# Gate products of a decoder layer: seven block products in place of eight, with keys and values in halves

## Chip, cores and metric

The kernel runs on one core of one Trainium2 chip. The metric is the device time of one execution in microseconds (us); the times shown are the median and the spread of three runs. All times below are in us unless ns is written.

## What is computed

A decoder layer on 2048 tokens of width 1024 in float32: one input projection, two causal mixers side by side, gates, a merge and a layer norm.

```python
h = x @ w_in + b_in          # columns: latents 544, z_a, u, v, z_b 512 each, g_a, g_b 1024 each
y_a = mla_attention(c_q, c_kv, k_pe) * silu(z_a)      # 8 heads, 96 wide for scores, 64 for values
y_b = spatial_gating(u, v) * silu(z_b)                # gelu(u) * (tril(w_s) layer_norm(gelu(v)) + b_s)
merged = sigmoid(g_a) * (y_a @ w_oa) + sigmoid(g_b) * (y_b @ w_ob)
x = layer_norm(2 ** 0.25 * x + merged @ w_out)
```

## The kernel before, in words

Every float32 product runs as three passes: `split` (L64) cuts an operand into a head (`hi`, a cast on ScalarE) and a rest (`lo`, a subtraction on VectorE), and `mm3` (L68) adds hi*hi, hi*lo and lo*hi in PSUM. The function has four stages.

- **Stage 1** makes the latents and q, k, v of 4 chunks of 512 tokens, and puts them in DRAM (`qnd`, `qrd`, `kd`, `krd`, `vd`).
- **Stage 2** makes v of the spatial gating unit (`gelu_v`, L375, tile `psa`), and mixes it (`mix`, L453): products `psm`, transposes `ptu`, copies `mo` on ScalarE, and writes of `mxd` by GpSimd's DMA queue. `mo` has two buffers.
- **The gates** (`gates`, L493): z_a, u, z_b, g_a and g_b are 28 column blocks of 128; each is a product of a 1024 x 128 piece of `w_feat` with x of 512 tokens, for 4 chunks: 28 x 4 groups of 8 k tiles x 3 passes, 2688 matmuls of 128 x 512 into tile `psg`, which has two PSUM banks (L408). `weights` (L496) loads a 512 KB piece (`fst`) and splits it (`fwh`, `fwl`) once for two chunks. `group` (L507) closes a bank after 24 matmuls: VectorE adds the bias (L522), or ScalarE takes the tanh (L518); `finish` (L527) does the rest of gelu and silu, and GpSimd's queue writes `fo` to `gd`. `gates` is a generator: one `next` issues one step of three matmuls. x is on chip for two chunks; `x_pieces` (L126) exchanges it halfway.
- **Stage 3, attention** (L575 to L767) per head and block of 256 queries (`Block`, L593): `score` (tiles of up to 512 keys in four banks `pss`, row maxima on VectorE, exponentials `pr` on ScalarE), `turn` (transposes `pt`, split into `ph` on ScalarE and `pl` on VectorE), `product` (with V into `po`). A loop at L716 sets TensorE's order by a clock of its own: each attention step is issued when what it waits for should be done (the `LAG_` constants, L53), and a step of `gates` (648 ns) goes in whenever no such step is due, or while the gates are owed time (`FILL`, L54). `keep_in_program_order` holds TensorE to that order. 48 gate steps go ahead of attention (L571), the rest of them after it. `head` (L582) loads K and V of a whole head into one of two buffers; a block's Q is loaded one block ahead (`block`, L706). Even heads take their blocks upward, odd heads downward (L696).
- **Stage 4** (from L774) multiplies by the gates, merges, projects by `w_out` and normalises; its first loads (`y`, `zb`, `o`, `z`, `r`) begin once attention has freed its memory, beside the last gate steps.

All loads are issued from SyncE's queue (SP), in order; `gd`, `mxd` and the attention output `otd` are written from GpSimd's queue (POOL).

Of the kernel before, what the change touches and what calls it, by code (L numbers as in the profile page):

```python
# [33 lines left out]
W = 512           # width of each mixer  # L34
C = 512           # tokens of a chunk
# [6 lines left out]
# inv_freq[i] = 10000 ** (-2 i / 32) in float32  # L42
# [15 lines left out]
def hybrid_layer_kernel(ctx, tc, xT, x, pos, invf, w_lat, b_lat, w_v, b_v,  # L58
# [37 lines left out]
    # by chunk: attention before its normalisation, mixed v, gates  # L96
# [5 lines left out]
    # ----------------------------------------------------------- constants  # L102
# [7 lines left out]
    # keep where q - k >= 0  # L110
# [7 lines left out]
    # x^T, two chunks of tokens on chip, each as (hi, lo)  # L118
    xp_cm = tc.tile_pool(name="xp", bufs=2, side="right")
# [4 lines left out]
    xt = {}  # L124

    def x_pieces(c):  # L126
        hi = xp.tile([P, KD, C], F32R, tag="xh", name=f"xh{c}")
        lo = xp.tile([P, KD, C], F32R, tag="xl", name=f"xl{c}")
        xt[c] = (hi, lo)
        for k in range(0, KD, 2):  # L130
            st = xs.tile([P, 2, C], F32, tag="st", name="xst")
            sp.dma_start(st, xT_v[:, k:k + 2, c * C:(c + 1) * C])
            for j in range(2):
                yield
                split(st[:, j, :], hi[:, k + j, :], lo[:, k + j, :])
# [5 lines left out]
    # ======================================================= 1: q, k and v  # L141
# [13 lines left out]
    hi0 = xp.tile([P, KD, C], F32R, tag="xh", name="xh0")  # L155
    lo0 = xp.tile([P, KD, C], F32R, tag="xl", name="xl0")
    for k in range(0, KD, 2):
# [6 lines left out]
        for j in range(2):  # L164
            split(st[:, j, :], hi0[:, k + j, :], lo0[:, k + j, :])
            split(ws[:, j, :], wlh[:, k + j, :], wll[:, k + j, :])
    xt[0] = (hi0, lo0)
# [5 lines left out]
    # rope tables: cos, sin of pos * inv_freq for all tokens  # L173
# [24 lines left out]
    # cos(r) = sin(pi/2 - |r|)  # L198
# [6 lines left out]
    # up projections, with the rms gains (and the score scale) folded in  # L205
# [21 lines left out]
    def rope(dst, src, t0, n, heads, nm):  # L227
        """dst[P, n*heads, 32] = rope(src); tables of token tiles t0 .. t0+n"""
# [16 lines left out]
    def latent(c, ts):  # L245
        """latents of token tiles ts: bias, rms norm, rope of k"""
# [8 lines left out]
        for k, t, h2 in order:  # L255
            tk = slice(t * P, (t + 1) * P)
            cs = slice(h2 * 272, (h2 + 1) * 272)
            mm3(pss[t, h2], (xh[:, k, tk], xl[:, k, tk]),
# [32 lines left out]
    def up(c, lh, ll):  # L291
        """k, v and q of a chunk, in four parts"""
# [16 lines left out]
        for t in range(4):  # L309
            tk = slice(t * P, (t + 1) * P)  # L310
            # q rope
# [8 lines left out]
            # k nope, head pairs  # L320
# [4 lines left out]
            # v  # L325
# [10 lines left out]
            # q nope, head pairs  # L336
# [24 lines left out]
    # ============================== 2: v of the spatial gating unit, mixed  # L361
# [572 lines left out]
```

## Time and profile before

| | |
|---|---|
| time, median of 3 runs (lowest to highest) | 1775.66 us (1775.54 to 1776.54) |
| span of the profiled execution | 1775.5 us |
| TensorE matmul busy | 1731.4 us, 98% |
| VectorE (DVE) busy | 1094.2 us, 62% |
| ScalarE (ACT) busy | 754.6 us, 43% |
| GpSimd (POOL) busy | 134.3 us, 8% |
| DMA | 229.06 MB, mean 129 GB/s |

The profiled execution's span and the median of the runs are 0.2 us apart: what lies around the span is small, and sums made against the span hold for the time. A matmul's shown duration overlaps that of the next, so a busy TensorE can still hide gaps of up to two tenths of a microsecond; the distance from one start to the next is what a matmul costs. Idle time in brackets stands before an instruction, with the one that ended it.

### The profile page before, as it was taken

What the parts mean: (1) busy time and instruction counts of PE and PEld (TensorE: products, weight loads), DVE (VectorE), ACT (ScalarE), POOL (GpSimd) and SP (SyncE); (2) the same over time, 40 slices, a digit from 0 to 9 for tenths busy, and PEclk for the clock granted to TensorE, in tenths of its full rate; (3) what the DMA queues carried; (4) which work ended last, traced back from release to release, by engine and by line L of the source; (5) the groups of instructions that cost most, each with busy time, mean ns of one, the idle gap of its engine ahead of it and who ended that gap; (6) DMA issues with size and microseconds to landing.
All of it is one profiled execution on the core that took longest, in us unless ns stands there. A gap on an engine that the chain in (4) does not pass through costs nothing.

```text
span 1775.5 us, 25048 instructions
## 1 busy us (share of the span) xinstructions
PE 1731.4 (98%) x9249; PEld 1484.1 (84%) x9249; DVE 1094.2 (62%) x2209; ACT 754.6 (43%) x1708; POOL 134.3 (8%) x231
## 2 busy tenths in 40 slices
PE   7999999899999999999999999999999999999998
PEld 7999887788888888888788888888888877888886
DVE  6765686476664555444776666654445478777664
ACT  6533442255544454545655445544544341303020
POOL 0000011100000100000100000100001000000000
PEclk9999999999999999999999999999999999999999
DMA  6564851631321422422713212321123886657341
GB/s 220 194 196 160 276 170 38 181 99 49 101 72 66 140 68 66 119 68 75 215 62 89 76 55 81 122 72 59 60 66 120 283 270 225 215 197 215 120 131 72
DMA packets 111100, 229.06 MB, mean 129 GB/s; under 512 B 13120, under 2 KB 41920, under 8 KB 108608
## 3 DMA queue, kind: packets, MB, share of 16 engines
q1 hardware_dynamic: 99968, 193.88, 34.9%
q0 software_dynamic: 11008, 33.57, 5.4%
q8 instruction: 73, 1.20, 0.3%
q14 instruction: 51, 0.42, 0.1%
HBM read 155.50 MB, written 71.89 MB: 128 GB/s over the span
## 4 chain that ended last, share of the span: by engine, by line
PE 45%; issue 41%; DMA 5%; POOL 4%; DVE 3%; ACT 2%; SPq 0%; POOLq 0%; DVEq 0%; ACTq 0%
PE po L86 11%; PE psg L86 9%; PE psa L86 4%; PE psl L86 4%; PE pb L86 4%; PE pa L86 4%; PE pss L86 3%; PE pt L658 2%; POOL gd L519 2%; DMA wost<-in_w_out_dram 1%; PE psq L86 1%; POOL otd L686 1%; DMA xst<-in_xT_dram 1%; DMA mxd<-mo 1%; PE psr L86 1%
## 5 line engine op out<-in xcount | busy, mean ns | idle before, releaser
L86 PE MATMUL psg<-xh,fwh 128*128 128x512 f32 x896 | 375.3, 419 | 4.9 <-DVE fo L522 4.9
L66 DVE TENSOR_TENSOR pl<-pt,ph 128x512 fp32r<-128x512 f32 (+2 forms) x352 | 199.7, 567 | 287.2 <-ACT ph L65 285.5
L86 PE MATMUL psg<-xl,fwh 128*128 128x512 f32 x896 | 354.5, 396 | 0.0
L86 PE MATMUL psg<-xh,fwl 128*128 128x512 f32 x896 | 354.1, 395 | 0.0
L65 ACT CAST ph<-pt 128x512 fp32r<-128x512 f32 (+2 forms) x352 | 172.0, 489 | 241.4 <-PE pt L658 208.8
L642 ACT ACTIVATE pr<-pss,nm 128x512 f32<-128x512 f32 (+2 forms) x320 | 198.0, 628 | 114.9 <-DVE nm L639 95.9
L86 PE MATMUL pss<-Kh,Q 96*128 96x512 f32 (+3 forms) x640 | 222.5, 377 | 12.9 <-DMA Q<-qrd 7.2
L86 PEld LDWEIGHTS psg<-xh,fwl 128*128 128x128 f32 x896 | 169.6, 189 | 38.4
L636 DVE TENSOR_REDUCE mx<-pss 128x1 f32<-128x384 f32 (+2 forms) x288 | 175.6, 619 | 29.4 <-PE pss L86 26.1
L86 PEld LDWEIGHTS psg<-xh,fwh 128*128 128x128 f32 x896 | 170.6, 190 | 25.6 <-issue 5.3
L86 PEld LDWEIGHTS psg<-xl,fwh 128*128 128x128 f32 x896 | 171.4, 191 | 20.7
L658 PE MATMUL pt<-ident,pr 128*128 128x128 f32 x1088 | 167.2, 274 | 0.0
L86 PEld LDWEIGHTS pss<-Kh,Q 96*128 96x128 f32 x640 | 119.3, 189 | 30.7 <-ACT pr L642 9.7
L658 PEld LDWEIGHTS pt<-ident,pr 128*128 128x128 f32 x1088 | 125.6, 141 | 5.8 <-ACT pr L642 0.4
L86 PEld LDWEIGHTS po<-ph,V 128*128 128x128 f32 x576 | 108.7, 189 | 26.0 <-ACT ph L65 3.2
L86 PE MATMUL pss<-Kl,Q 96*128 96x512 f32 (+2 forms) x320 | 115.9, 362 | 0.0
L86 PE MATMUL po<-pl,V 128*128 128x256 f32 x576 | 113.9, 279 | 0.2
L86 PE MATMUL po<-ph,V 128*128 128x256 f32 x576 | 112.8, 276 | 1.2 <-DVE o L685 0.7
L86 PEld LDWEIGHTS po<-pl,V 128*128 128x128 f32 x576 | 96.5, 190 | 11.3 <-DVE pl L66 1.2
L86 PE MATMUL po<-woh,mh 128*128 128x512 f32 x256 | 100.8, 394 | 1.2 <-ACT mh L65 1.2
L86 PE MATMUL po<-woh,ml 128*128 128x512 f32 x256 | 100.4, 393 | 0.0
L86 PE MATMUL po<-wol,mh 128*128 128x512 f32 x256 | 99.7, 390 | 0.0
(208 smaller groups left out, 2986.3 us busy)
## 6 DMA issues: line engine op xcount, KB each, us to landing
fst<-in_w_feat_dram SPq DMA_DIRECT2D x56, 512.0 KB, 3.7
gd<-fo POOLq DMA_DIRECT2D x96, 256.0 KB, 2.3
wabst<-in_w_ab_dram SPq DMA_DIRECT2D x32, 512.0 KB, 4.2
xst<-in_xT_dram SPq DMA_DIRECT2D x31, 512.0 KB, 4.9
kd<-e SPq DMA_DIRECT2D x16, 512.0 KB, 3.2
vd<-ve SPq DMA_DIRECT2D x16, 512.0 KB, 4.1
qnd<-e SPq DMA_DIRECT2D x16, 512.0 KB, 4.7
Q<-qnd SPq DMA_DIRECT2D x64, 128.0 KB, 2.9
```

Of the source, the lines that this page charges most:

```text
L65: act.copy(hi, src)
L66: dve.tensor_tensor(lo, src, hi.bitcast(F32), op=ALU.subtract)
L86: inorder(pe.matmul(*args, **kw))
L519: pool.dma_start(gd[c][m], o)
L636: dve.tensor_reduce(self.mx[:, i:i + 1], ps[:, :n], axis=AX.X, op=ALU.max)
L642: act.activation(pr[:, k0:k0 + ne], pe_[:, :ne], AF.Exp, bias=self.nm, accum_out=ls[:, self.h, 2 * self.qc + j, e:e + 1])
L658: inorder(pe.transpose(pt[:, i, j * P:(j + 1) * P], self.pr[j][:, (k + i) * P:(k + i + 1) * P], ident))
L686: pool.dma_start(otd[self.qc // 2][self.h * DV:(self.h + 1) * DV, self.qc % 2 * 256:(self.qc % 2 + 1) * 256], o2)
```

## The change

The 28 column blocks are paired into 14 units, and a unit, two halves of the 1024-long contraction and two chunks of tokens make 2 x 2 blocks on either side of the product. Sums and differences of blocks of the weights (p6, p3, p7) and of x (T1 to T4) give the four results by seven block products instead of eight, with three partial sums p1, p1+p6 and p1+p6+p5. For each pair of chunks (two passes `p`) there are two sweeps over the units: z=0 makes p1, p6, p5, p3 in one bank, one on top of the other, copies the three partial sums out to DRAM (`rawd`) and finishes one result; z=1 makes p7, p4 and p2, and adds the partial sum that it loads back. Two units alternate on the two banks. A block product is 4 k tiles x 3 passes, 12 matmuls: 14 x 2 x 7 x 12 = 2352.

K and V are loaded in halves of the keys (the second half has one buffer), Q has three buffers and comes two blocks ahead, all heads take their blocks upward, a row's score tiles end at key 1024, and u is no longer multiplied by z_b on the way: stage 4 loads `u` and multiplies.

```diff
-MT_ORDER = [m for f in range(4) for m in (MT_U + f, MT_ZB + f, MT_ZA + f)] + list(range(MT_GA, MT))
-FILL = 1.19       # time of the gates' products per time of the attention's
+_UZ = [m for f in range(4) for m in (MT_U + f, MT_ZB + f, MT_ZA + f)]
+_GM = list(range(MT_GA, MT))
+UNITS = [(m, _GM[n]) for n, m in enumerate(_UZ)] + [(_GM[12], _GM[13]), (_GM[14], _GM[15])]
+UNITS = UNITS[:6] + UNITS[12:13] + UNITS[6:12] + UNITS[13:]
+FILL = 1.03
+    rawd = [[dram.tile([3, P, C], F32, name=f"rw{p}_{n}") for n in range(MT // 2)] for p in range(2)]
...
+    def x_sum(p, what, slot, of=None):
...
+        for k in range(4):
+            a, b = nxt
+            if k < 3:
+                nxt = fetch(k + 1)
+            v = a[:, 0]
+            if what == "T1":
+                dve.tensor_tensor(v, a[:, 1], v, op=ALU.subtract)
+            elif what == "T3":
+                dve.tensor_tensor(v, v, a[:, 1], op=ALU.subtract)
+            elif b is not None:
+                dve.tensor_tensor(v, v, b[:, 1], op=ALU.subtract)
+                dve.tensor_tensor(v, v, b[:, 0], op=ALU.add)
+            elif what in ("T2", "T4"):
+                for e in xc[p, {"T2": "T1", "T4": "T2"}[what]]:
+                    dve.tensor_tensor(v, v, e[:, k, :].bitcast(F32), op=ALU.subtract)
+            split(v, hl[0][:, k, :], hl[1][:, k, :])
+            yield
...
+        def load(p, z, n, e):
+            m1, m2 = UNITS[2 * n + e]
+            st = []
+            for m in (m1, m2):
+                t = fw.tile([P, KD, P], F32, tag="fst", bufs=4, name="fst")
+                sp.dma_start(t, w_feat[m])
...
+            elif q == "p6":
+                dve.tensor_tensor(a22, a22, a21, op=ALU.add)
+                yield
+                dve.tensor_tensor(a21, a22, a11, op=ALU.subtract)
+                cut(key, a21)
...
+            if q in ("p1", "p6", "p5"):
+                o = fq[0].tile([P, C], F32, tag="fo", bufs=3, name="fo")
+                act.copy(o, ps)
+                pool.dma_start(rawd[p][u][("p1", "p6", "p5").index(q)], o)
+                return
...
+            else:
+                m, c = {"p2": (m1, c1), "p4": (m2, c1), "p7": (m2, c2)}[q]
+                o = kept.pop(key)
+                if m < MT_GA:
+                    dve.scalar_tensor_tensor(o, ps, bft[:, m:m + 1], o, op0=ALU.add, op1=ALU.add)
+                else:
+                    dve.tensor_tensor(o, ps, o, op=ALU.add)
...
+            if i + 3 < len(prods):
+                jobs = prepare(prods[i + 3])
...
+                    t = fq[0].tile([P, C], F32, tag="fo", bufs=3, name="fo")
+                    sp.dma_start(t, rawd[pp_][2 * n4 + e4][{"p2": 0, "p4": 1, "p7": 2}[q4[4]]])
...
+            if i + 5 < len(prods) and prods[i + 5][4] == PASS[prods[i + 5][1]][0]:
+                load(*prods[i + 5][:4])
...
+        first = gates(fw, fq, ps_g)
+        next(first)
         mix(*pend)
...
+    fq_cm = tc.tile_pool(name="fq", bufs=2, side="right")
+    fq.append(fq_cm.__enter__())
+    for _ in range(47):
         next(fill)
...
-        order = [(h, qc if h % 2 == 0 else 7 - qc) for h in range(H) for qc in range(8)]
+        order = [(h, qc) for h in range(H) for qc in range(8)]
...
-                if n % 8 == 1 and h + 1 < H:
-                    hds[h + 1] = head(h + 1)
+                if qc == 2:
+                    hds[h, 1] = head(h, 1)
+                if qc == 4 and h + 1 < H:
+                    hds[h + 1, 0] = head(h + 1, 0)
...
+                u = wa.tile([P, C], F32, tag="r", name="u")
+                sp.dma_start(u, gd[c][MT_U + f])
                 dve.tensor_tensor(y, y, z, op=ALU.mult)
+                dve.tensor_tensor(y, y, u, op=ALU.mult)
```

Counted over the built programs: gate matmuls 2688 to 2352; loads of `fst` 56 to 112; splits of weights (`fwh`, `fwl`) 112 to 196; new on VectorE 112 sums of weight blocks, 48 sums of x, and 84 additions that close a bank (against 48 biases before); splits of x 64 to 96; new on ScalarE 84 copies that close a bank, and 24 with the bias; new on GpSimd's queue 84 writes of `rawd` and 16 of `gd`; new on SP 84 loads of `rawd`. The score tiles have the same number of columns in all, 24 more matmuls of them are 128 wide, and 48 more are 256 wide.

The order on TensorE at the end of stage 2 (`ptu` is the last transpose of the mixing, `psg` with its number a bank's use by one group or unit). Before:

```order
L472 MATMUL ptu_3511<-ident_78,um_3454 128x128 x4
L472 MATMUL ptu_3519<-ident_78,um_3454 128x128 x4
L86 MATMUL psg_3573<-xl1_2967,fwh_3535 128x512
L86 MATMUL psg_3573<-xh1_2966,fwl_3536 128x512
L86 MATMUL psg_3573<-xh1_2966,fwh_3535 128x512
...
L86 MATMUL psg_3615<-xh0_2940,fwh_3609 128x512
```

Now:

```order
L90 MATMUL psg_3632<-xh0_2976,fwh_3536 128x512
L90 MATMUL psg_3632<-xl0_2977,fwh_3536 128x512
...
L708 MATMUL ptu_3607<-ident_106,um_3550 128x128 x4
L708 MATMUL ptu_3615<-ident_106,um_3550 128x128 x4
L90 MATMUL psg_3632<-xh1_3304,fwh_3546 128x512
L90 MATMUL psg_3632<-xl1_3305,fwh_3546 128x512
```

Before, groups with banks of their own followed the last transpose; now the first product after it (p6) adds into the bank that p1 has filled ahead of it, which is to be copied out first.

The order on VectorE amid attention (`pl` is attention's split, `mx` and `nm` its maxima; `fst`, `fwl` and `fo` are the gates'). Before:

```order
L66 TENSOR_TENSOR pl<-pt,ph 128x512
L636 TENSOR_REDUCE mx<-pss 128x1
L522 TENSOR_SCALAR fo<-psg,bft 128x512
L66 TENSOR_TENSOR fwl<-fst,fwh 128x512 x2
L545 SCALAR_TENSOR_TENSOR fo<-ft,fo 128x512
L66 TENSOR_TENSOR pl<-pt,ph 128x512
L547 TENSOR_TENSOR fo<-fo,gu 128x512
```

Now:

```order
L70 TENSOR_TENSOR fwl<-fst,fwh 128x512
L70 TENSOR_TENSOR pl<-pt,ph 128x512
L455 TENSOR_TENSOR fst<-fst 128x512
L457 TENSOR_TENSOR fst<-fst 128x512
L455 TENSOR_TENSOR fst<-fst 128x512
L462 TENSOR_TENSOR fst<-fst 128x512
L70 TENSOR_TENSOR pl<-pt,ph 128x512
L522 TENSOR_TENSOR fo<-psg,fo 128x512
L70 TENSOR_TENSOR fwl<-fst,fwh 128x512
```

Sums of freshly loaded weights now stand between attention's splits.

The order on SP at a change of heads (`Kl`, `Kh`, `V` are a head's keys and values). Before:

```order
L588 DMA Kl_10012<-kd_59 64x2048
L588 DMA Kh_10011<-kd_59 64x2048
L589 DMA Kh_10011<-krd_60 32x2048
L589 DMA Kl_10012<-krd_60 32x2048
L603 DMA Q_10019<-qnd_57 64x2x256
```

Now:

```order
L759 DMA Kl_6816<-krd_60 32x1024
L437 DMA fst_6517<-in_w_feat_dram 128x1024
L758 DMA Kh_6375<-kd_59 64x1024
L759 DMA Kh_6375<-krd_60 32x1024
L758 DMA Kl_6376<-kd_59 64x1024
L759 DMA Kl_6376<-krd_60 32x1024
L773 DMA Q_6383<-qnd_57 64x2x256
```

The weights' loads now stand between the halves of K.

## Rows read from the trace of the kernel before

**Rows 1.** Time windows: PE, PEld, DVE, ACT, POOL busy (instructions), TensorE clock, DMA share, GB/s.

```profile
307.00:1412.00 1105.00, 1085.28 (x5934) 937.92 (x5933) 633.24 (x1275) 546.53 (x1326) 91.41 (x167) 0.99 0.32 98
339.00:1366.00 1027.00, 1011.85 (x5591) 877.85 (x5591) 595.66 (x1213) 522.76 (x1287) 81.96 (x150) 0.99 0.28 86
```

**Rows 2.** Timeline of PE, gate matmuls: start, duration.

```profile
329.76 0.39 PE L86 MATMUL psg<-xh,fwl 128*128 128x512 f32 x1
...
334.52 0.39 PE L86 MATMUL psg<-xh,fwl 128*128 128x512 f32 x1
...
644.41 0.40 PE L86 MATMUL psg<-xh,fwl 128*128 128x512 f32 x1
...
645.80 0.39 PE L86 MATMUL psg<-xh,fwl 128*128 128x512 f32 x1
```

**Rows 3.** Timeline of PE, the end of stage 2.

```profile
319.65 1.14 PE L472 MATMUL ptu<-ident,um 128*128 128x128 f32 x8
...
339.77 0.76 PE L86 MATMUL psg<-xh,fwh 128*128 128x512 f32 x1 [4.87 <-DVE fo L522]
340.34 0.63 PE L86 MATMUL psg<-xl,fwh 128*128 128x512 f32 x1
...
345.03 0.63 PE L86 MATMUL psg<-xh,fwh 128*128 128x512 f32 x1
```

**Rows 4.** Chain that ended last, the same place.

```profile
326.86 10.82 DMA mxd<-mo
```

**Rows 5.** Waits: who for whom, us in total, times, longest.

```profile
DVE pl L66 <- ACT ph L65: 285.5, 199, 2.3
...
DVE ls L691 <- DMA mxd<-mo: 8.5, 1, 8.5
...
PE pss L86 <- DMA Q<-qrd: 7.2, 3, 3.1
```

**Rows 6.** Timeline of PE at a change of heads.

```profile
611.56 0.41 PE L86 MATMUL pss<-Kh,Q 96*128 96x384 f32 x1 [3.13 <-DMA Q<-qrd]
...
613.50 0.63 PE L86 MATMUL psg<-xh,fwh 128*128 128x512 f32 x1
613.93 0.63 PE L86 MATMUL psg<-xl,fwh 128*128 128x512 f32 x1
```

**Rows 7.** Groups by line, VectorE: count | busy us, mean ns | idle before.

```profile
L66 DVE TENSOR_TENSOR pl<-pt,ph 128x512 fp32r<-128x512 f32 x224 | 154.5, 690 | 227.6 <-ACT ph L65 226.5
L66 DVE TENSOR_TENSOR fwl<-fst,fwh 128x512 fp32r<-128x512 f32 x112 | 75.1, 686 | 28.1 <-ACT fwh L65 27.7
L522 DVE TENSOR_SCALAR fo<-psg,bft 128x512 f32<-128x512 f32 x48 | 35.9, 748 | 18.1 <-PE psg L86 17.2
```

**Rows 8.** Groups by line, ScalarE.

```profile
L65 ACT CAST fwh<-fst 128x512 fp32r<-128x512 f32 x112 | 66.7, 622 | 38.0 <-PE psg L86 37.6 <-DMA fst<-in_w_feat_dram 0.4
L518 ACT ACTIVATE fo<-psg,bfh 128x512 f32<-128x512 f32 x64 | 44.2, 690 | 26.3 <-PE psg L86 26.3
L474 ACT COPY mo<-ptu 128x512 f32<-128x512 f32 x16 | 9.0, 587 | 23.5 <-PE ptu L472 15.9 <-DMA mxd<-mo 7.6
```

**Rows 9.** Time windows of 10 us amid attention, columns as in rows 1.

```profile
860.00:870.00 10.00, 8.80 (x48) 7.55 (x49) 7.68 (x20) 6.03 (x17) 1.13 (x3) 1.00 1.01 344
870.00:880.00 10.00, 10.00 (x57) 8.57 (x56) 9.36 (x22) 9.75 (x27) 1.20 (x3) 1.00 0.66 213
880.00:890.00 10.00, 9.41 (x52) 7.96 (x51) 8.33 (x19) 6.14 (x17) 0.52 (x1) 1.00 0.55 167
```

**Rows 10.** DMA issues: KB of each, median us from issue to landing.

```profile
fst<-in_w_feat_dram SPq DMA_DIRECT2D x56, 512.0 KB, 3.7
gd<-fo POOLq DMA_DIRECT2D x96, 256.0 KB, 2.3
```

**Rows 11.** Timeline of PE and ACT, a group's last matmul and its closing.

```profile
578.80 0.40 PE L86 MATMUL psg<-xh,fwl 128*128 128x512 f32 x1
...
582.66 0.70 ACT L518 ACTIVATE fo<-psg,bfh 128x512 f32<-128x512 f32 x1
```

More of the change, by code (lines that the diff above doesn't have):

```diff
@@ L123, in hybrid_layer_kernel, with x_slot, x_new @@
     xT_v = xT.rearrange("(k p) s -> p k s", p=P)
-    xt = {}
+    xt, x_half = {}, {}
+    def x_slot(n):
+        return tuple(xp.tile([P, KD // 2, C], F32R, tag=f"x{e}{n}", name=f"x{e}{n}") for e in "hl")
+    def x_new(c):
+        hv = [x_slot(2 * (c % 2) + e) for e in range(2)]
+        x_half[c, 0], x_half[c, 1] = hv
+        xt[c] = tuple([hv[k // 4][e][:, k % 4, :] for k in range(KD)] for e in range(2))
+        return xt[c]
     def x_pieces(c):
-        hi = xp.tile([P, KD, C], F32R, tag="xh", name=f"xh{c}")
-        lo = xp.tile([P, KD, C], F32R, tag="xl", name=f"xl{c}")
-        xt[c] = (hi, lo)
+        hi, lo = x_new(c)
         for k in range(0, KD, 2):
@@ L134, in x_pieces @@
                 yield
-                split(st[:, j, :], hi[:, k + j, :], lo[:, k + j, :])
+                split(st[:, j, :], hi[k + j], lo[k + j])
     def load_x(c):
@@ L359, in hybrid_layer_kernel, with fetch @@
     lctx.close()
+    xc = {}
+    def x_sum(p, what, slot, of=None):
+        if what == "T4":
+            hl = xc[p, "T2"]
+        else:
+            hl = x_slot(slot)
+        xc[p, what] = hl
+        c1, c2 = (slice((2 * p + e) * C, (2 * p + e + 1) * C) for e in range(2))
+        src = {"B11": ((0, c1),), "B21": ((4, c1),), "T4": ((4, c1),), "B22": ((4, c2),),
+               "T1": ((0, c1), (0, c2)), "T3": ((4, c2), (0, c2)), "T2": ((4, c2),)}[what]
+        def fetch(k):
+            a = xs.tile([P, 2, C], F32, tag="st", name="xa")
+            for n, (d, cs) in enumerate(src):
+                sp.dma_start(a[:, n], xT_v[:, k + d, cs])
+            b = None
+            if what == "T2" and of is None:
+                b = xs.tile([P, 2, C], F32, tag="st", name="xb")
+                sp.dma_start(b, xT_v[:, k, 2 * p * C:(2 * p + 2) * C].rearrange("p (a b) -> p a b", a=2))
+            return a, b
+        nxt = fetch(0)
+        yield
[16 more added lines that the diff above has]
+            yield
@@ L485, in hybrid_layer_kernel @@
                 norm(vh, vl, t, *(early[t] if c == 2 else gelu_v(c, t)))
+                if c == 1:
+                    next(t2)
                 if c == 3 and t == 1:
@@ L490, in hybrid_layer_kernel @@
             pend = (c, vh, vl)
+        assert next(t2, None) is None
+        first = gates(fw, fq, ps_g)
+        next(first)
         mix(*pend)
[L493 to L568 removed]
@@ L570, in hybrid_layer_kernel @@
-    fill = gates()
-    for _ in range(48):
+    fill = first
+    fq_cm = tc.tile_pool(name="fq", bufs=2, side="right")
+    fq.append(fq_cm.__enter__())
+    for _ in range(47):
         next(fill)
@@ L581, in hybrid_layer_kernel, with head @@
         ps_o = ph.enter_context(tc.tile_pool(name="p3O", bufs=1, space=PSUM))
[L582 to L591 removed]
+        def head(h, half):
+            ks = slice(half * S // 2, (half + 1) * S // 2)
+            Kt = [kp.tile([DH, S // 2], F32R, tag=f"K{e}{half}", bufs=2 - half, name=f"K{e}") for e in "hl"]
+            Vt = kp.tile([P, NT // 2, 2 * DV], F32R, tag=f"V{half}", bufs=2 - half, name="V")
+            for sl in (slice(0, 512), slice(512, S // 2)) if h == 0 and half == 0 else (slice(0, S // 2),):
+                dl = slice(half * S // 2 + sl.start, half * S // 2 + sl.stop)
+                for i, K in enumerate(Kt):
+                    sp.dma_start(K[:DN, sl].bitcast(F32), kd[h // 2, h % 2 * DN:(h % 2 + 1) * DN, i, dl])
+                    sp.dma_start(K[DN:, sl].bitcast(F32), krd[:, i, dl])
+            sp.dma_start(Vt.bitcast(F32), vd[h][:, half * NT // 2:(half + 1) * NT // 2, :])
+            return Kt + [Vt]
         class Block:
@@ L610, in __init__ @@
                     nb = 2 * qc + j + 1
-                    nt = -(-nb // 4)
-                    ends = [-(-nb * (i + 1) // nt) * P for i in range(nt)]
+                    ends = []
+                    for lo, hi in ((0, min(nb, 8)), (8, nb)):
+                        nt = -(-(hi - lo) // 4)
+                        ends += [(lo + -(-(hi - lo) * (i + 1) // nt)) * P for i in range(nt)]
+                    nt = len(ends)
                     self.todo += [(j, i, k0, k1 - k0, i == nt - 1)
@@ L708, in block @@
                 h, qc = order[n]
-                if n % 8 == 1 and h + 1 < H:
-                    hds[h + 1] = head(h + 1)
+                if n == 0:
+                    hds[0, 0] = head(0, 0)
+                if qc == 2:
+                    hds[h, 1] = head(h, 1)
+                if qc == 4 and h + 1 < H:
+                    hds[h + 1, 0] = head(h + 1, 0)
                 blocks[n] = Block(h, qc, hds)
-        block(0)
-        block(1)
+        for n in range(3):
+            block(n)
         while vi < len(order):
@@ L746, in hybrid_layer_kernel @@
                     si += 1
-                    block(si + 1)
+                    block(si + 2)
             if cost:
@@ L767, in hybrid_layer_kernel @@
         keep[0] = False
+    fq_cm.__exit__(None, None, None)
     psg_cm.__exit__(None, None, None)
```

238 lines of the change are left out of this document (146 added, 92 removed).

## The prediction

> **What bounds the kernel now.** I read the time windows first, for the share of each engine in the attention stage; then TensorE's timeline, for what a matmul costs from start to start; then waits and chain, for what the few idle stretches hang on; last the groups by line, for durations.
>
> Over the stretch that holds gates and attention TensorE is busy 1011.85 of 1027 us [rows 1]: 15.15 us idle, 0.15 in 10. VectorE is at 58% (595.66), ScalarE at 51%. So TensorE bounds, and a matmul that goes is time that goes, as long as nothing else becomes late. A gate matmul costs (334.52 - 329.76) / 21 = 0.2267 us ahead of attention and (645.80 - 644.41) / 6 = 0.2317 amid it [rows 2]; the durations shown (0.39) overlap and are no price. The granted clock is 0.99 [rows 1].
>
> The idle stretches are few. At the end of stage 2 TensorE stands 4.87 us, for the closing of a bank [rows 3]; that closing hangs on a write of `mxd` that takes 10.82 us to land [rows 4]. At three changes of heads it waits for Q, 7.2 us in all [rows 5], and the gate matmuls right behind such a wait stand 0.43 apart in place of 0.23 [rows 6]: half the clock, 1.2 GHz, after the idle. The wait after which VectorE has idled longest is for `ph`, 285.5 us over 199 times [rows 5]. It costs TensorE nothing while the two split and the gates fill, but it shows that VectorE, which works in order, often stands at an instruction that is not ready.
>
> **The change part by part, against the span of 1775.5 us** (0.2 us from the median of the runs, so the sum holds for both).
>
> *Matmuls removed.* 2688 - 2352 = 336, by the mean of the two spacings, 0.229: **-77** (bounds -76.2 and -77.8, by either spacing). The Trainium skill, "TensorE: Matmul & The Clock Gate", section "Back-to-back issue gap", has one matmul follow the next after N/2.4 GHz plus some 2.5 ns, 216 ns for 512 columns. By that the term would be -72.5 and the sum 4.5 us higher; the spacings here are 11 to 16 ns longer, so the measured one is taken.
>
> *End of stage 2.* The last transposes are issued at 319.65 and take 1.14 [rows 3], to 320.8. Before, groups with banks of their own filled most of what follows. Now p6 comes next and adds into p1's bank, whose copy to `fo` has first to be made; `fo` is in memory that the `mo` buffers held, so the copy waits for the last `mxd` write: 326.86 + 10.82 = 337.7 [rows 4], and a copy of 128x512 takes 0.59 [rows 8]. So TensorE stands 337.7 + 0.6 - 320.8 = 17.5 in place of 4.87: **+13**. Bounds: +5, if the write starts 8 us sooner because fewer gate steps share the queues and engines then, and +17, if the copy stands 4 us behind other work on ScalarE. Before, 11 matmuls ran at half the clock after the idle (0.426 each [rows 3]); that comes again after the longer idle, and costs nothing new.
>
> *VectorE and ScalarE amid attention.* New on VectorE: 84 splits `fwl` at 0.686 [rows 7], 58; 112 sums of weight blocks, of the same shape and so priced alike (estimate 0.69), 77; some 40 of the sums of x, 28; some 28 splits of x, 19; 84 closings at 0.69 less 48 biases at 0.748 [rows 7], 22; less 16 multiplications that moved to stage 4, -11. Together 192 over 633 [rows 1], 825 us. The stage of 1105 us [rows 1] loses 77 of its matmuls, so this is 80% of 1028, where 57% was. ScalarE gets 84 casts at 0.622, 84 copies at 0.587, 28 casts of x and 24 tanh or bias passes at 0.690 [rows 8]: 136 over 546.5, 66%.
>
> None of it is on the path as long as it is ready ahead: the weights are prepared three products ahead, and a product amid attention lasts 1028 / 196 = 5.2 us on average, 2.8 (12 x 0.23) where the gates run alone. What happens when VectorE is that full shows in the fullest windows of the old stage: at 77%, 94% and 83% VectorE TensorE idles 1.20, 0 and 0.59 of 10 us [rows 9], 0.6 on average at 85%. At 80% I take 0.4 in 10, nearer to these windows than to the 0.15 of today, as 80% is nearer to 85% than to 58%. Over some 950 us of attention that is 38, less the 15 that are lost now: **+23**. In the 15 are the 7.2 us of Q waits, which go: Q is now loaded two blocks ahead. Bounds: -15, if nothing idles, and 1.2 in 10 throughout, 114 - 15 = +99.
>
> A second cover is the bank. A unit's next product adds into the same bank, so its copy has to be over within the other unit's product; before there were 24 matmuls for a closing, now 12. The closing of one group amid attention ended 582.66 + 0.70 - 578.80 - 0.23 = 4.3 us after its last matmul [rows 11], near 5.2; this is a long one, and it is part of why I don't take the -15.
>
> *The tail.* 13 products stand after the last attention product, on three `fo` buffers. One use of a buffer: load 3.7 (by the nearest load [rows 10], of twice the size), the other unit's product 2.8, closing 0.75, write 2.3 [rows 10], 9.5; three products last 8.4. At some four uses of each buffer, 4 x 1.1: **+4** (0 if the load starts early; 13 if each use pays three times that).
>
> *Stages 2 and 4, and the scores.* 12 of the x sums (8 us of VectorE) fall into stage 2; stage 4 gets 16 loads and moves 16 multiplications, 11 us, into itself. Both lie beside TensorE's work there: **+3** (0 to 11). 72 more score matmuls for the same columns, at 0.229 less 512 columns at 2.4 GHz, 16 ns, is **+1** (6.4 if a narrow one cost as much as a wide one: 24 x 128 + 48 x 256 columns).
>
> *At nothing*: the 84 `rawd` and 16 `gd` writes more on GpSimd's queue, which is busy 91 of 1105 us [rows 1] and lands a write in 2.3 us [rows 10]; the halves of K and V, the same bytes in more loads.
>
> Sum: 1775.5 - 77 + 13 + 23 + 4 + 3 + 1 = **1742.5**. With all bounds at one end 1688 and 1846.
>
> **The rivals.**
>
> *A, the whole gain.* The covers hold: VectorE's new work fits into the 285.5 us that it now waits for `ph` [rows 5], and TensorE keeps only the stand at the end of stage 2. For it: the windows at 94% lose nothing [rows 9]. Against it: the neighbours lose 0.6 to 1.2. 1775.5 - 77 + 13 - 7 (Q) = **1704.5**, from 1690 to 1715.
>
> *B, slower: VectorE stands at a weight sum whose load is late.* Before, a load was issued a whole double group ahead. Now a pair of loads is issued as a product ends, one product before its sums are prepared: some 5 us, where a load takes 3.7 alone [rows 10]. At a change of heads it stands on SP behind a half of K or V, and such loads have made Q late by up to 3.1 us [rows 5]; windows exist in which the DMA engines are full (share 1.01 [rows 9]), and the stage's traffic grows. Then VectorE, in order, holds the `pl` that is queued behind the sum, and attention's products and TensorE wait for `pl`. 56 pairs of loads at 1.5 us, half of that longest Q wait, are 84 in place of the 23: **1803.5**. It decides from 1.0 us a pair (56 / 56). Against it: most pairs come amid blocks where no K is loaded, at a DMA share of 0.28 [rows 1], and then 5 us are enough for 3.7.
>
> *C, late writes.* The `rawd` writes of GpSimd's queue land late once VectorE is full, so the three `fo` buffers come free late. Landing 2.3 us [rows 10] becomes 5 (bound: the 10.82 of [rows 4]); amid attention a product's 5.2 us cover most of that, in the tail 2.7 us more at four uses of a buffer are 11: 4 + 11 in place of 4, **1753.5**. The Trainium skill, "SBUF — State Buffer", section "SBUF: two separate sides", warns that VectorE can block the making of GpSimd's descriptors, and has a transfer go from 620 to 3100 ns by it. No row here shows that: writes land in 2.3 us beside a VectorE at 57%.
>
> *The change doesn't do what it says* can be left out: the counts and orders ahead of this prediction are those of the built programs.
>
> **How the numbers follow.** Forecast, 1715 to 1770: 0.57. A: 0.20. B: 0.13. C: 0.04, inside the forecast's band but by another cause. Between the forecast and B, 1770 to 1783: 0.06. A measurement can tell 0.2%, 3.5 us, from no change. Faster than 1772.1: 0.57 + 0.20 + 0.04 + 0.01 of the gap = 0.82. The same: 0.04 of the gap and 0.01 of B, 0.05. Slower: 0.13. The range reaches from 1703, which leaves out the lower half of A (0.09), to 1783, which leaves out most of B (0.11).
>
> **What would show it.** 784 gate groups of three matmuls in place of 896; the stretch of 1105 us at some 1070; after the last `ptu` one stand of TensorE of 15 to 19 us, ended by a copy of ScalarE; no wait for Q; VectorE at about 80% there; 36 to 40 us from the last `po` of attention to the last gate matmul. If TensorE idles under 10 us amid attention, A is right. If VectorE's waits show `fst` on its loads with tens of us, and TensorE's show `pl` behind it, B is right. If `fo` waits on `rawd` writes that take 5 us or more, C is right. The forecast is wrong in its largest term if the gate matmuls' spacing amid attention is not 0.23, or if the idle per 10 us there lies outside 0.2 to 0.8.

## The result, and the profile after

The changed kernel takes 1828.79 us (median of 4 runs, 1823.36 to 1830.51) against 1775.6 for the kernel before: ratio 1.0295, 95% interval 1.0279 to 1.0311. It is 53 us slower. I had forecast 1742.5, and 1783 as the upper end.

The head of the page after, with VectorE up from 1094.2 to 1268.7 us, ScalarE from 754.6 to 877.0, and TensorE's matmul time down only from 1731.4 to 1702.6, in a longer span:

```profile
PE 1702.6 (93%) x8913; PEld 1438.2 (79%) x8913; DVE 1268.7 (69%) x2521; ACT 877.0 (48%) x1932; POOL 188.8 (10%) x331
```

Time windows after, columns as in [rows 1]: the attention stage, and the gate matmuls left behind it.

```profile
346.00:1401.00 1055.00, 990.78 (x5374) 842.82 (x5375) 733.08 (x1463) 636.29 (x1500) 133.85 (x246) 0.98 0.51 159
...
1400.00:1453.00 53.00, 42.17 (x160) 32.63 (x161) 32.34 (x53) 18.62 (x30) 7.03 (x13) 0.90 0.82 269
```

TensorE is idle for 64.2 of 1055 us, where it was idle for 15.15 of 1027 [rows 1]. VectorE is at 69%, not at the 80% that I had reckoned, mainly because the stage is longer: between 307 and 1453 us, from the gates' first stretch to their last, it works 785 of 1146 us, where I had 825 of 1028. The granted clock's mean over the span fell from 0.992 to 0.972.

The busy time of a pipelined matmul hides small gaps, so I use one measure for all that follows. From TensorE's timeline I take each matmul's distance to the next start, less the median distance of its kind (same tile and shape), and add that up over a stage. This is called the excess here; half clock after an idle stretch is in it. The stages end at the last `ptu`, the first `pss`, the last matmul of attention, and the last gate matmul.

| excess, us | stages 1, 2 | to first `pss` | attention | tail | stage 4 | span |
|---|---|---|---|---|---|---|
| before | 17.5 | 7.5 | 32.3 | -0.8 | 5.1 | 1775.5 |
| changed | 34.4 | 13.2 | 108.4 | 15.7 | 17.8 | 1828.5 |
| difference | +16.9 | +5.7 | +76.1 | +16.5 | +12.7 | +53.0 |

The five differences make +127.9; with the -77 of the removed matmuls that is +51, which leaves 2 of the 53 open. The median spacing of a gate matmul is 0.231 us in both, so the matmuls themselves did not become dearer. What they gave was lost in every stage, most of it in attention.

There TensorE waits for what VectorE and ScalarE make. Waits, columns as in [rows 5], the first line before and the others after:

```profile
PE pss L86 <- ACT pr L642: 5.4, 6, 2.2
```

```profile
DVE pl L70 <- ACT ph L69: 125.3, 128, 3.0
...
PE pss L90 <- ACT pr L814: 33.0, 29, 2.9
...
DVE fst L455 <- DMA fst<-in_w_feat_dram: 30.2, 18, 4.5
...
DVE fst L466 <- DMA fst<-in_w_feat_dram: 23.9, 18, 2.8
...
PE po L90 <- DVE pl L70: 18.8, 18, 3.9
```

VectorE's idle time at `ph` has fallen from 285.5 us to 125.3, and TensorE now stands 33.0 us for `pr`, where it stood 5.4, and 18.8 for `pl`. No wait of TensorE for Q is left. VectorE stands 54 us at sums of weights, 36 times. The longest of these, on VectorE, SP and TensorE:

```profile
870.82 0.69 DVE L457 TENSOR_TENSOR fst<-fst 128x512 f32<-128x512 f32 x1
876.06 0.69 DVE L455 TENSOR_TENSOR fst<-fst 128x512 f32<-128x512 f32 x1 [4.55 <-DMA fst<-in_w_feat_dram]
876.67 0.69 DVE L462 TENSOR_TENSOR fst<-fst 128x512 f32<-128x512 f32 x1
877.27 0.68 DVE L70 TENSOR_TENSOR pl<-pt,ph 128x512 fp32r<-128x512 f32 x1
```

```profile
869.71 0.33 SPq L586 DMA_DIRECT2D fo<-rw  x1
870.13 0.70 SPq L437 DMA_DIRECT2D fst<-in_w_feat_dram  x1
```

```profile
878.01 0.79 PE L90 MATMUL po<-pl,V 128*128 128x256 f32 x2 [3.94 <-DVE pl L70]
```

The load goes out at 870.13, VectorE comes to its sum at 871.5 and stands until 876.06; `pl` is two instructions behind, and TensorE stands 3.94 us for it. This is the picture of rival B. What it is worth was a matter for experiments.

### The profile page after: what moved, and what is told of

It reads as the page before. It is cut to its first block, busy times and chain, and to the rows that moved or that the text cites. A ratio compares the mean times of both kernels' runs of the same rounds, so it can differ in the third digit from the quotient of the medians.

```text
span 1828.5 us, 25939 instructions
## 1 busy us (share of the span) xinstructions
PE 1702.6 (93%) x8913; PEld 1438.2 (79%) x8913; DVE 1268.7 (69%) x2521; ACT 877.0 (48%) x1932; POOL 188.8 (10%) x331
## 4 chain that ended last, share of the span: by engine, by line
issue 42%; PE 34%; DMA 8%; POOL 6%; DVE 6%; ACT 3%; POOLq 0%; SPq 0%; DVEq 0%; ACTq 0%
PE po L90 10%; PE psg L90 5%; PE pa L90 4%; PE pb L90 4%; PE psl L90 4%; DMA fst<-in_w_feat_dram 2%; POOL rw L508 2%; PE pss L90 2%; POOL gd L480 1%; PE psa L90 1%; POOL otd L858 1%; PE psq L90 1%; POOL gd L496 1%; PE pt L830 1%; DMA wabst<-in_w_ab_dram 1%
## 5 line engine op out<-in xcount | busy, mean ns | idle before, releaser
L90 PE MATMUL psg<-xh,fwh 128*128 128x512 f32 x784 | 332.9, 425 | 19.6 <-ACT fo L507 10.6
L90 PE MATMUL psg<-xh,fwl 128*128 128x512 f32 x784 | 314.0, 401 | 0.0
L90 PE MATMUL psg<-xl,fwh 128*128 128x512 f32 x784 | 313.7, 400 | 0.0
L70 DVE TENSOR_TENSOR pl<-pt,ph 128x512 fp32r<-128x512 f32 (+2 forms) x352 | 199.1, 566 | 127.9 <-ACT ph L69 125.3
L808 DVE TENSOR_REDUCE mx<-pss 128x1 f32<-128x512 f32 (+3 forms) x288 | 174.3, 617 | 39.0 <-PE pss L90 37.7
L90 PEld LDWEIGHTS psg<-xh,fwh 128*128 128x128 f32 x784 | 152.2, 194 | 43.7 <-ACT fo L507 11.0
L90 PEld LDWEIGHTS psg<-xh,fwl 128*128 128x128 f32 x784 | 150.7, 192 | 34.6
L69 ACT CAST fwh<-fst 128x512 fp32r<-128x512 f32 x196 | 122.2, 626 | 106.3 <-PE psg L90 86.5
L90 PEld LDWEIGHTS psg<-xl,fwh 128*128 128x128 f32 x784 | 152.6, 195 | 22.4
L70 DVE TENSOR_TENSOR fwl<-fst,fwh 128x512 fp32r<-128x512 f32 x196 | 134.2, 686 | 49.7 <-ACT fwh L69 46.7
L90 PE MATMUL po<-pl,V 128*128 128x256 f32 x576 | 119.1, 288 | 19.3 <-DVE pl L70 18.8
```

Source lines behind the costliest of these rows:

```text
L69: act.copy(hi, src)
L70: dve.tensor_tensor(lo, src, hi.bitcast(F32), op=ALU.subtract)
L90: inorder(pe.matmul(*args, **kw))
L808: dve.tensor_reduce(self.mx[:, i:i + 1], ps[:, :n], axis=AX.X, op=ALU.max)
```

## Experiments

Theory 1: VectorE stands at late loads. Theory 2: VectorE and ScalarE have too much to do between attention's links. Theory 3: the upward order of heads costs time. Theories 4 and 5 are told in the expectations of e7 and e15. The excess amid attention (attn) stands beside each time, from one profiled execution. Kernels that ran once are compared by differences of 10 us and more; e9, e12, e13, e14 and e16 ran four times.

**e1, the loads.** The two units' tiles are loaded once, and sums become maxima of the same shape.

```diff
-            st = []
-            for m in (m1, m2):
...
+            st = held.setdefault(e, [])
+            if not st:
+                for m in (m1, m2):
...
-                dve.tensor_tensor(a22, a22, a21, op=ALU.add)
+                dve.tensor_tensor(a22, a22, a21, op=ALU.max)
...
```

> The changed kernel without 108 of its 112 weight loads: each of the two units' pairs of tiles is loaded once and used over and over, and the four sums are maxima of the same shape, so the weights of all later units are left out. Theory 1 (late loads: VectorE stands 54 us at sums whose load is issued only when a buffer comes free, and holds pl and the maxima behind it): the stand goes, the excess of TensorE amid attention falls from some 110 us to 30 to 50, time 1750 to 1775 us. Theory 2 (VectorE and ScalarE are simply too full, and the steps come later than the planner's lags allow): at most 20 us come back, time 1808 us or more. Theory 3 (the upward order of all heads): nothing comes back.

1771.38 us, 57 less than the changed kernel; attn 59.5 in place of 108.4. The time is in theory 1's range, the excess above its 30 to 50. But the edit takes away four things at once: the stand, the bytes, the wait for buffers, and the order that follows from them.

**e2, the sums.** The four sums of `prepare` are left out, the loads stay.

> The changed kernel with all loads but without the 112 sums of weight blocks on VectorE (77 us of its work; the products then have plain blocks of the weights). Theory 1: loads are as late as before, and VectorE or ScalarE stands for them at the splits; under 15 us come back, 1815 us or more. Theory 2: VectorE falls from 70% to 63% of the attention stage, and 30 to 50 us come back, 1780 to 1800 us. Theory 3: nothing comes back.

1774.35 us, attn 61.9: as much as e1, which theory 1 had not said. VectorE has no wait for `fst` left, ScalarE waits 2.8 us for it at the casts. With the sums their stands went too, so this run doesn't tell the theories apart.

**e5, both edits.**

> Both edits at once: the weights of the first two units are used over and over, and no sums of weights are made. Theory 1 (what cost the time was that VectorE stood at late loads; the 77 us of sums by themselves are nearly free): the two edits take away the same stand, so no more comes back than with one of them, 1760 to 1772 us. Theory 2 (the two gains of 57 and 54 us are two things, late loads and VectorE's work): they add up, 1715 to 1735 us.

1759.72 us, attn 50.0. The gains of 57 and 54 don't add up; they are largely one thing. With no load to wait for, 77 us of sums cost 9.5 us of excess (59.5 to 50.0). So the busy time of the sums by itself accounts for an eighth of the 76; the rest of VectorE's new work, and ScalarE's, was not taken out. It can be read the other way round too: with no sums to make, the 108 loads cost 12 us (61.9 in e2 to 50.0). Both edits together take off 58, so 37 of them come only where loads and sums are there at once.

**e3 and e12, the order of heads.** The kernel before, with `order = [(h, qc) for h in range(H) for qc in range(8)]`.

> The kernel before with one edit: all heads take their blocks upward. Theory 3 (at a head's change the longest block now stands before the shortest, and the chain of a short block is exposed): 15 to 40 us slower than before, 1790 to 1815 us. Theories 1 and 2: within 5 us of before, up to 1781 us.

> The kernel before with all heads upward, timed: it was 14 us faster in one look. All theories: faster than both kernels, 1755 to 1763 us, with no wait for Q left at the heads' changes.

1759.13 us once (e3); over four runs (e12) 1761.11 us, ratio to before 0.9908 (0.9881 to 0.9935). Theory 3 falls, with the sign reversed: upward alone is some 14 us faster than the kernel before, its attn is 17.7 (e12) in place of 32.3, and no wait for Q is left. This one line beats both kernels.

**e4, longer lags in TensorE's order.** `LAG_S` to `LAG_O` 2300, 900, 2300, 3100, 2300.

> The changed kernel with the planner's lags half as long again (1500, 700, 1500, 2100, 1500 ns become 2300, 900, 2300, 3100, 2300), so that more gate steps go between the steps of attention that wait for each other. Theory 2: the idle amid attention falls by a third or more, 25 to 45 us back, 1785 to 1805 us. Theory 1: the stands at loads stay, under 12 us back, or nothing. Theory 3: some 10 us back, at the heads' changes alone.

1980.08 us. No theory had that. More gate steps went between the links, and the gates ran out at 1240 us; the last 341 us of attention had no filler:

```profile
1241.00:1582.00 341.00, 264.31 (x1134) 209.36 (x1132) 154.10 (x329) 137.25 (x367) 11.98 (x23) 0.73 0.12 34
```

**e18, the filler.** The changed kernel with 14 matmuls per block product in place of 12: two are issued twice, so the sums differ.

```diff
+                    if j == 1 and k in (1, 2):
+                        mm(ps, a[:, k, :], b[:, k, :], start=False, stop=False, skip_group_check=more)
```

> The changed kernel with 14 matmuls in place of 12 in each block product (two are issued twice, so that the sums are not the gates'): as many gate matmuls as the kernel before (2744 against 2688), all else as in the changed kernel. If TensorE's work bounds as before: 392 x 0.229 = 90 us slower, 1915 us or so. If the removed matmuls were the filler that hid attention's links, and their time has only become idle time: under 45 us slower, below 1873 us, with the excess amid attention well under 100.

1868.88 us: 392 more matmuls, 90 us of TensorE's time by their spacing, cost 40. The excess amid attention falls to 68.8, though VectorE still stands 52 us at sums. In the changed kernel over half the price of a gate matmul goes into time that is idle anyway. Read the other way round, each of the 392 that are taken out to come back to the changed kernel brings some 0.10 us, not 0.229; taking out further ones was not tried.

**e6, the sums on GpSimd.** `dve.` becomes `pool.` in the four sums.

> The changed kernel whole, with the 112 sums of weight blocks on GpSimd in place of VectorE, so that GpSimd and not VectorE stands at a late load. Theory 1: the stand leaves VectorE, 35 to 55 us come back, 1775 to 1795 us, if GpSimd makes a sum in under 2 us and its writes of fo are not held up by it. Theory 2: as much, by the 77 us of work that leave VectorE. A third way: GpSimd works through its queue in order and the writes of partial sums then land late, and the time stays above 1815 us.

1801.03 us, attn 76.3; 28 come back, less than the 35 to 55 of either theory. GpSimd takes 1.29 us for a sum, and its waits name the stand that VectorE had:

```profile
POOL fst L466 <- DMA fst<-in_w_feat_dram: 75.9, 21, 7.1
...
POOL fst L455 <- DMA fst<-in_w_feat_dram: 47.6, 19, 5.0
```

**e9, loads earlier.** Each of the four blocks gets tiles of its own (`fst0` to `fst3`, two buffers each, the same memory), and a block's successor is loaded once its last split is emitted.

> The changed kernel whole, in the same memory, but each of a unit's four weight blocks has a tile of its own (two buffers each), the fourth sum (for p3) is made right behind p6's, and a block's successor is loaded as soon as that block's own last split is emitted: the two blocks that the first sums need come four products or more ahead in place of being loaded with the last freed one. Theory 1 (the time went where VectorE stands at weights that are loaded only when the last buffer comes free): VectorE's waits for fst fall from 54 us under 10, the excess amid attention from 108 to about 60, 1770 to 1790 us. Theory 2: sums and splits are as many, so under 20 us come back, 1810 us or more.

1804.03 us (ratio to before 1.0150, 1.0127 to 1.0174), attn 91.3; 25 us come back. But VectorE still stands 41 us at its sums:

```profile
DVE fst L473 <- DMA fst<-in_w_feat_dram: 16.9, 11, 5.1
DVE fst L467 <- DMA fst<-in_w_feat_dram: 14.6, 13, 2.9
...
DVE fst L463 <- DMA fst<-in_w_feat_dram: 9.6, 9, 2.2
```

The scheduler that orders its queue seems to have moved the sums forward with the loads; e13 and e16 bear that out. So the lead of the load alone does not end the stands, and the 17 us of attn came with only 13 us of stands gone.

**e13, the sums in order.** Only `inorder(...)` around the four sums, which holds each behind what the program writes ahead of it.

> The changed kernel whole, with the four sums of weight blocks held on VectorE behind what the program writes ahead of them (before, the scheduler that orders VectorE's queue placed them as early as it reckoned the load to be there). Theory 1, as it stands now (not the load is late but the sum stands too early in VectorE's order): VectorE's waits for fst fall from 54 us under 15, the excess amid attention from 108 to 60 to 75, 1780 to 1797 us. If loads are late whatever the order: VectorE waits as long at the same sums, and the time stays above 1815 us.

1806.84 us (1.0181, 1.0150 to 1.0212), attn 93.4. On VectorE the stands are gone, down from 54 us to 7:

```profile
DVE fst L455 <- DMA fst<-in_w_feat_dram: 4.4, 1, 4.4
DVE fst L466 <- DMA fst<-in_w_feat_dram: 2.9, 3, 2.4
```

Holding the sums took off 15 us amid attention, and some 20 in all; I had expected 30 to 50 of the time back. (The profiled execution was the slowest of the four.) TensorE's wait for `pl` halves, from 18.8 to 9.3 us, and that for `pr` stays at 33.0. Part of the stand seems to have moved only: ScalarE's casts of weights now wait 38 us for sums, where they waited 18. Theory 1 is right that the place of a sum makes VectorE stand and that time hangs on it. But e9 gained as much with 41 us of stands left, so the stands' own price for TensorE is not settled by e13.

**e14 and e16, quarter loads and sums in order** (e14 with four `fo`, for which `o1` and `o2` have one buffer each).

> The kernel with quarter loads and four fo buffers, and the sums held in order as well. Theory 1 as it stands now: VectorE's waits for fst go to under 5 us, the excess amid attention to 55 to 65, and with the tail's 6 to 8 us the time is 1765 to 1780 us, near the kernel without repeated loads (1771) with all the work done. If quarter loads bring nothing on top: as with the sums in order alone, less 6 us.

> The changed kernel with quarter loads and the sums held in order, but with two o1 and two o2 buffers again (with one each, VectorE stood up to 3 us for the write of an attention output). If that stand was what the four-fo kernels lost in attention: excess amid attention 75 to 85 in place of 92, 1780 to 1793 us. If not: within 5 us of the kernel with four fo, 1795 to 1805 us.

1799.68 and 1796.76 us (e16: 1.0115, 1.0094 to 1.0135); attn 91.7 and 88.6, far from the 55 to 65 expected of e14. In e16 VectorE waits 2.7 us for `fst`: from e9 to e16 38 us of stands go, and 3 us of attn. Two `o1` and `o2` again, with three `fo`, changed attn by 3 us, so their buffers were not what attention lost. So the changed kernel's full work, with no stand at a load, is still 20 us slower than before.

**e17, the bytes.** e1, with every saved load made as a copy of the same 512 KB from DRAM to DRAM.

```diff
+                    inorder(sp.dma_start(sink[e][k], w_feat[m]))
```

> The kernel without repeated loads, but each load that it saves is made as a copy of the same 512 KB from DRAM to DRAM at the same place of SP's order, with no reader and no buffer to wait for (so the bytes also go out once more). If the bytes on the DMA engines are what made links late (x, Q, partial sums and writes landing later): 15 to 30 us slower than without repeated loads, 1786 to 1802 us. If it is the buffers and the order alone: within 8 us of it, 1763 to 1779 us.

1787.80 us, attn 70.4: 16 and 11 us more than e1, at the low edge of what was expected of the bytes. The copy writes them too, so I take the 11 as the most that the loads' bytes cost amid attention; the 12 that the loads cost without sums (e2 to e5) agree.

**e7, fewer waits for weight buffers** (e1 with weights prepared two products ahead).

> The kernel without repeated loads, in which weights are prepared two products ahead in place of three: one of the four fwh and fwl buffers is then always free when a cast comes up. Theory 4 (of what remains amid attention, 42 us above the kernel before with upward blocks, a good part is ScalarE that stands at a cast of weights until TensorE frees the buffer, 87 us of waits, with pr and ph behind it): 15 to 30 us less than without repeated loads, 1741 to 1756 us. If it is the number of instructions that stand between nm, pr and pl: within 8 us of it, 1763 to 1779 us.

1769.52 us, attn 58.5, no change. But ScalarE waits for `fwh` buffers as long as in e1, 89.5 us against 87.4, so the edit did not take away what theory 4 blames, and theory 4 stays untested.

**e15, all gate work in order.**

> The same kernel, with all of the gates' work on VectorE and ScalarE held in the order of the program (splits, sums of x, copies and closings too). Theory 5 (what remains amid attention, 42 us above the kernel before with upward blocks, comes from gate work that is placed ahead of nm, pr or pl before its operand is there): 15 to 30 us less than with the sums alone held, 1740 to 1760 us. Theory 2 (it is the number of instructions between attention's links): within 8 us of it, either way.

1814.34 us, attn 108.8: the fixed order costs 17 us of attention against e14, where theory 5 had 15 to 30 less. It is no better an order, though: VectorE waits 55.9 us at `fwl` for casts, 43.4 in e14. So theory 5's remedy fails, and that placement matters is not excluded. The scheduler's freedom is worth something for splits and closings, and costs something for the sums.

**e8, the end of stage 2** (a tile of `ft` taken ahead of the first `fo`) **and e10, e11, the tail** (`fo` with four buffers, alone and on top of e9).

> The changed kernel with one tile of ft taken from its pool ahead of the first fo, so that the fo buffers no longer lie in the memory of the mo buffers and the first copies of partial sums need not wait for the last writes of mxd. If the wait at the end of stage 2 is the landing of those writes: the stand of 10.95 us there falls under 3 us and the time by 8 to 14 us, 1815 to 1821 us. If the order of TensorE is the cause whatever the memory: within 3 us of the changed kernel.

> The changed kernel with four fo buffers in place of three (o1 and o2 with one in place of two, for the memory). If the last gate products stand for fo buffers that come free late: the excess of TensorE between the end of attention and the last gate matmul, 15.7 us, falls under 7, and SP's waits for gd writes ahead of a partial sum's load fall from 224 us to less than half; 1815 to 1822 us. If that tail stands for the order of closings on VectorE and ScalarE instead: within 4 us of the changed kernel.

> Both of these edits in one kernel. If they are independent: the sum of their gains against the changed kernel, within 5 us.

e8: 1828.55 us, no change; the stand is 9.40 us in place of 10.64, and the copy still waits for `mxd`. Whether `fo` had left that memory is not shown. e10: 1823.33 us, as the fastest of the changed kernel's own runs; the tail's excess falls from 15.7 to 9.4, not under 7, and SP's waits for `gd` writes only from 224 to 196 us. The fourth buffer may be worth 6 us of the tail, but e5 has 9.4 there with three, so this is not shown. e11: 1803.17 us, 1 us from e9 alone and 5 from the sum of both gains; its tail is 7.4, but attention loses 8 us against e9, where `o1` and `o2` had two buffers.

## Why the prediction was wrong

**The step that failed first** is the opening one: "a matmul that goes is time that goes, as long as nothing else becomes late". A gate matmul had two uses, its product and the time that it gives to attention's links. The -77 was real as TensorE's time, and the spacing held. But 336 matmuls of filler went while the links grew longer. From the start of a row's last score matmul to the end of its `nm` it took 3.2 us at the ninth decile before and 4.5 after (means 2.2 and 3.0, by the two timelines), where the order on TensorE reckons with 1.5 behind the matmul (`LAG_S`). e18 shows the exchange: matmuls put back cost under half their price. e4 shows the other end, where the filler is gone.

**The term "+23" amid attention measured +76.** I took the idle time from three full windows of the old stage [rows 9] by VectorE's busy share. VectorE is at 70% amid attention now, under the 80% of the working, and yet more was lost. Time windows of attention, before and after, columns as in [rows 1]:

```profile
353.00:1366.00 1013.00, 998.62 (x5547) 867.14 (x5545) 589.05 (x1203) 519.84 (x1282) 80.34 (x147) 0.99 0.28 85
```

```profile
375.00:1401.00 1026.00, 962.31 (x5262) 819.52 (x5261) 721.82 (x1446) 623.27 (x1477) 128.46 (x236) 0.98 0.51 158
```

By the idle time that I had counted, TensorE loses 63.7 us, 0.62 in 10: more than the 0.4 of the sum, but inside the 0.2 to 0.8 outside which I had called the term wrong. The excess is 1.06 in 10, for it counts also what the shown durations hide and the matmuls at half clock. So a busy share doesn't price the loss, and idle time sizes it too low.

The upward order by itself takes 14.6 us off (32.3 to 17.7, e12), so there are 108.4 - 17.7 = 91 to account for. Loads and sums together are 58 of them (108.4 to 50.0, e5): 12 that the loads cost without sums, about what e17 allows their bytes; 9.5 that the sums cost without loads; and 37 that come only from both. Of these, holding the sums in order takes 15 off (e13), by whatever way; 22 stay open, and earlier loads, which bring 17 by themselves (e9), bring only 5 more once the sums are held (e16). The last 32 are there with neither loads nor sums (50.0 in e5): 84 more casts, splits and closings stand between the links, and 336 fewer matmuls cover them; those two were not told apart, and theory 4 (casts that wait for a buffer) is still open. Nor was the pace of the gates (`FILL`, lowered from 1.19 to 1.03 with the rest) tried alone.

The **+1** for scores was a misreading: both kernels issue 960 score matmuls, more of them narrow and more of them full, so there are no 72 more.

**"End of stage 2, +13" measured +22.6** (16.9 and 5.7 of the table).

```profile
333.93 1.97 PE L708 MATMUL ptu<-ident,um 128*128 128x128 f32 x8 [0.51 <-ACT mo L710]
346.54 0.80 PE L90 MATMUL psg<-xh,fwh 128*128 128x512 f32 x1 [10.64 <-ACT fo L507]
```

```profile
340.44 0.58 ACT L710 COPY mo<-ptu 128x512 f32<-128x512 f32 x1 [6.08 <-DMA mxd<-mo]
342.50 0.58 ACT L710 COPY mo<-ptu 128x512 f32<-128x512 f32 x1 [1.48 <-DMA mxd<-mo]
345.90 1.07 ACT L507 COPY fo<-psg 128x512 f32<-128x512 f32 x2 [2.81 <-DMA mxd<-mo]
```

The chain is the one predicted, copy behind the `mxd` write, and the stand is shorter than the 17.5 that I gave. What I missed lies ahead of it: the last transposes of the mixing come 15 us later (335.5 against 320.5). TensorE stands there for `um` and `vh`; the cast `vh` is queued behind a copy that waits for an earlier `mxd` write, and the first `um` behind sums of x (`xa`) on VectorE:

```profile
304.70 0.58 PE L90 MATMUL psm<-vh,wsh 128*128 128x256 f32 x1 [3.86 <-DVE um L701]
...
323.32 0.80 PE L90 MATMUL psm<-vh,wsh 128*128 128x256 f32 x2 [4.08 <-ACT vh L69]
...
331.02 2.40 PE L708 MATMUL ptu<-ident,um 128*128 128x128 f32 x8 [1.67 <-DVE um L704]
```

```profile
322.17 0.59 ACT L710 COPY mo<-ptu 128x512 f32<-128x512 f32 x1 [3.09 <-DMA mxd<-mo]
322.65 0.62 ACT L69 CAST vh<-gv 128x512 fp32r<-128x512 f32 x1
```

```profile
302.69 0.69 DVE L405 TENSOR_TENSOR xa<-xa 128x512 f32<-128x512 f32 x1 [1.23 <-DMA xa<-in_xT_dram]
303.30 0.68 DVE L619 TENSOR_TENSOR gv<-psa,bv 128x512 f32<-128x512 f32 x1
303.90 0.75 DVE L701 TENSOR_TENSOR um<-psm,sgg 128x256 f32<-128x256 f32 x2
```

So sums of x in stage 2, which I had put beside TensorE's work, can stand on its path. Counted on TensorE's timeline, 96 gate matmuls stood among and right behind the last mixing before; now there are 24, one product for each of the two banks.

**"The tail, +4" measured +16.5.** TensorE stands at closings that wait for VectorE, as here:

```profile
1419.41 0.47 PE L90 MATMUL psg<-xh,fwh 128*128 128x512 f32 x1 [3.47 <-DVE fo L522]
...
1441.78 0.80 PE L90 MATMUL psg<-xh,fwh 128*128 128x512 f32 x1 [3.06 <-DVE fo L522]
```

Waits after, from 1396 to 1460 us:

```profile
DVE fo L522 <- DMA fo<-rw: 6.9, 4, 3.2
...
DVE fo L520 <- DMA fo<-rw: 3.3, 1, 3.3
```

VectorE itself waits there for partial sums, 10.2 us, which are loaded when an `fo` buffer comes free. I had reckoned one such round trip at 1.1 us more than its cover. With a fourth buffer the excess was 9.4 (e10); the rest was not taken apart.

**"Stages 2 and 4, +3":** stage 4 alone measured +12.7, among it 2.14 us for `yah`, whose operand `o` VectorE gets late: it waits 1.22 us for the load of `o`.

```profile
1456.77 0.69 DVE L998 TENSOR_TENSOR o<-o,r 128x512 f32<-128x512 f32 x1 [1.22 <-DMA o<-otd]
```

```profile
1458.89 0.50 PE L90 MATMUL pa<-yah,wabh 128*128 128x512 f32 x1 [2.14 <-ACT yah L69]
```

Its excess was between 7 and 19 over kernels with the same stage 4; it wasn't taken apart.

**The rivals.** B had the sign and the mechanism, with a chance of 0.13. VectorE stood 54 / 56 = 0.97 us per pair of loads, where B had 1.5, but holding the sums gave TensorE only 15 us back amid attention. The cause was another: the load is not stuck behind K or V but goes out when VectorE frees the buffer, as SP's waits show, and the sum stands too early in VectorE's order (e13).

```profile
SPq L437 <- DVE fwl L70: 269.0, 66, 15.9
```

I also let B stand in place of the +23, where both hold at once. A, the whole gain, needed the covers to hold; they did not. C: writes land later, `rw` and `gd` 3.5 us against 2.3 [rows 10], but not because VectorE is full. In e1 VectorE does as much in less time (720 us in its 976 of attention, 722 in 1026 after) and they land sooner. After, then e1:

```profile
gd<-fo POOLq DMA_DIRECT2D x112, 256.0 KB, 3.5
rw<-fo POOLq DMA_DIRECT2D x84, 256.0 KB, 3.5
```

```profile
gd<-fo POOLq DMA_DIRECT2D x112, 256.0 KB, 2.7
rw<-fo POOLq DMA_DIRECT2D x84, 256.0 KB, 2.3
```

This speaks against C's mechanism here. The warning of the Trainium skill ("SBUF — State Buffer", section "SBUF: two separate sides"), which led me to weigh C, is for VectorE in a two-port mode; I had left that condition out, and no run here shows such a mode. The Q waits went as predicted, and e12 shows that the upward order alone does that.

## What to carry to other kernels

Where one engine's spare work fills the waits of a chain on others, cutting that work is worth less than its length: price it by issuing some of it twice, as e18 did on the changed kernel; the same can be done on the old one before the cheaper form is built. A busy share tells whether an engine bounds, not how late a link comes; measure the link (here from score to `nm`) against the lag that the order reckons with. When two edits bring 49 and 47 alone and 58 together, no share belongs to one of them: tell what each costs without the other, and what only both make. And when a scheduler orders a queue, look where it puts the first user of a transfer: an instruction that stands too early holds all that is queued behind it, and an earlier load left 41 of the 54 us of stands (e9).

## What the hardware showed that I had not expected

With the gates gone, attention alone got a granted clock of 0.73 over 341 us (e4), with TensorE busy for 264 of them; beside the gates it is 0.99 [rows 1] and 0.98 in the changed kernel. Here the filler thus also went with the upper of the two clock levels. And writes of partial sums of the same size from GpSimd's queue landed in 2.3 us without the repeated weight loads beside them (e1) and in 3.5 us with them, at the same work on VectorE.
